# Hybrid attention layer on one core: the last unit's accumulating transfers issued with its evacuation, scan operands loaded later, a low-rank tail in four steps

## The chip, the cores and the metric

The kernel runs on one core of a Trainium2 chip. The metric is the device time of one execution in microseconds (us). The matrix engine is called PE (PEld is its loading of weights), the vector engine DVE, the scalar engine ACT, the GpSimd engine POOL, and the engine that only issues transfers here SP. L12 is line 12 of the kernel before.

## What is computed

One encoder layer over 512 tokens of width 2048, all in float32:

```
h = rmsnorm(x);  proj = h @ w_in              # 2048 x 6176
aq, ak, av, gq, gk, gv, gr, glr = split(proj)
attn = sum over 3 dilation patterns of windowed attention, 16 heads x 64
log_a = log_sigmoid(glr @ gate_w + gate_b) / 16    # low rank: 16 per direction
o = gated_linear_scan(gq, gk, gv, log_a_f) + the same backwards, 4 heads
gla = rmsnorm(o) * norm_w * silu(gr)
x = x + concat(attn, gla) @ w_out
x = x + (silu(h2 @ w_gate) * (h2 @ w_up)) @ w_down;  final rmsnorm
```

## The kernel before

Every float32 product is made of three PE matmuls of rounded parts (high x high, high x low, low x high). So each weight half and each activation is split: ACT casts the high part (L237 for weights) and DVE subtracts to get the low part (L218).

All engines' instruction streams are written in one order by hand; each engine executes its own stream in order, and waits are put in by tile. Small tiles of 512 columns (`s2`, 36 of them, "a" in the profile) and large ones of 1024 (`s4`, 33, "b") are handed out first in, first out; a tile that is handed out again makes its writer wait until the last user of it is done. `s2.free.rotate(14)` puts the 14 most recently freed first.

The stages around the change:

- **The first projection** (`Front.run`): 14 units (gate, scan q/k, attention q/k columns of `w_in`), each of four pieces q = 0 to 3, computed by a seven-product scheme into seven PSUM banks. After a unit's last piece `evac7` is a generator: its first step copies and adds the banks into `c` and three leftovers r1, r2, r3 (L1562 to L1570 and the adds through L1556, L1557); its second step adds once more (L1556 again, the line of the helper) and lets POOL issue four accumulating transfers that add r1, r2 and r3 onto `c` (L1581 to L1584; the last two touch halves that the first two write, and so wait for them); then it idles some turns and `finish` scales the unit by the norm (L1683) and stores it to `qkd`, `grd` or `gfd` from POOL (L1684). The last unit's `finish` is kept aside as `fr.late`.
- During the last unit, piece 1 issues `read_qk(0)` (eight POOL transfers of q and k of the first head pair, L569), and piece 2 issues `gla_operands`: the low-rank weights from SP, and two gate matrices (memset L792, transfer L793) and two reset rows (L794) from POOL.
- **The next jobs** (`run_job`) are ordinary projections, first that of a part of the scans' q and k: 16 weight halves i = 0 to 15, two to a loaded piece, each used for four output blocks, with 12 matmuls for each half (L337 to L339). At most three pieces are held in order of issue; SP loads them (L209). Between the blocks, a credit of 3.1 turns for a half runs the side work, one step at a turn: `run_urgent` first gives the oldest entry of the list `urgent` one step, and then the first entry of `side` gets one.
- `side` begins with `slow(low_rank())` and then `attention()`. `slow` doubles every step. `low_rank` splits the low-rank weights, multiplies in four steps (L818, L819), and in the step of the last eight matmuls also does the whole tail: copy from PSUM (L825), add (L826), scale (L827), and `stacked`, that is two casts on ACT (L800) and a subtraction on DVE (L801). Two more steps do `stacked` for the two gate matrices.
- `attention()` walks 64 units (16 heads x 4 blocks of queries), two steps for a unit: scores (L630, L631), bias added and maximum (DVE L640, which writes a small tile), exponential (ACT L648), scaling (L653 on DVE, L657 on ACT), transposes (PE L662), rounding (ACT L670) and low part (DVE L676), and the product with the values (L686, L687). Bias lines come by SP (L552), values by SP in `load_v` (L600), q and k are rounded by `load_qk` (ACT L592, DVE L588).
- Then the linear-attention scans, the output projection and the feed-forward part.

The hook `before_first(i)` of the first job inserts `load_qk(0)` at half 1, `load_v(0)` at half 2 and `fr.late()` at half 9.

Of the kernel before, what the change touches and what calls it, by code (L numbers as in the profile page):

```python
# [112 lines left out]
def put(*slots):  # L113
    for s in slots:
        if s.home is not None:
            s.home.free.append(s.i)


def layer(nc, tc, x, attn_norm_w, w_in, rel_table, gw_f, gb_f, gw_b, gb_b, gla_norm_w, w_out,
# [7 lines left out]
    with tc.manual_schedule(), \  # L127
# [9 lines left out]
        def hilo(keep=0):  # L137

            if len(s2.free) >= 2 + keep and (len(s2.free) >= 2 * len(s4.free) or not s4.free):
                return s2.get(F32R), s2.get(F32R)  # L140
            return s4.pair()
# [120 lines left out]
        urgent = deque()  # L262

        def run_urgent():
            while urgent:
                try:
                    next(urgent[0])
                    break
                except StopIteration:
                    urgent.popleft()  # L270
# [289 lines left out]
        def read_qk(pr):  # L560

            f = 1 - pr % 2
            if pr < NH // 2:
                qkr[pr] = [[s2.get(F32R) for _ in range(2)] for _ in range(2)]
                for i in range(2):
                    for n in range(2):
                        src = qkd[pr // 2 * 2 + i][64 * n:64 * n + 64, f * 512:(f + 1) * 512]
                        for r in (slice(0, 64), slice(64, 128)):
                            pool.dma_start(out=qkr[pr][i][n].f[r], in_=src)  # L569
# [26 lines left out]
        def load_v(half, ts=range(4)):  # L596
            for t in ts:
                v = s4.get(F32R, [P, 8, 2, DH])
                VS.setdefault(half, []).append(v)
                sp.dma_start(out=v.f.rearrange("p h s c -> p (h s c)"), in_=vd[4 * half + t])  # L600
# [111 lines left out]
        def attention():  # L712


            def run(f, u, n=UNITS):
                if 0 <= u < n:
                    f(u)

            for u in range(UNITS + 7):
                h = u // 4  # L720
                if u < UNITS:
                    if u % 8 == 1:
                        read_qk(h // 2 + 1)
                    if u % 8 == 4 and h // 2 + 1 < NH // 2:
                        urgent.append(slow(load_qk(h // 2 + 1)))
                    while h // 2 not in ready:
                        run_urgent()
                run(att_scores, u)
                run(att_scale, u - 3)
                run(att_round, u - 4)  # L730
                run(att_exp, u - 1)
                if u % 2:
                    run(att_lift, (u - 7) // 2, UNITS // 2)
                mixed = None
                if "mix" in at:
                    pr = at.pop("mix")
                    f, (hi, lo) = mixf.pop(pr), s4.pair() if pr > 4 else hilo()
                    act.copy(hi.t, f.t)
                    mixed = pr, f, hi, lo
                yield  # L740
                run(att_norm, u - 2)
                run(att_transpose, u - 3)
                if u % 2 == 0:
                    run(att_av, (u - 6) // 2, UNITS // 2)
                run(att_rest, u - 4)
                run(att_max, u)
                if u % 2:
                    run(att_mix, (u - 7) // 2, UNITS // 2)
                if mixed:
                    pr, f, hi, lo = mixed  # L750
                    dve.tensor_tensor(lo.t, f.t, hi.f, op=OP.subtract)
                    put(f)
                    mixh[pr] = hi, lo
                if 34 <= u < 37:
                    load_v(1, ((0,), (1,), (2, 3))[u - 34])
                if u == UNITS - 3:
                    load_gla(0)
                yield
# [17 lines left out]
        def slow(steps):  # L776
            for _ in steps:
                yield
                yield


        G = {}
# [3 lines left out]
        def gla_operands():  # L786
            G["raw"] = s2.get(F32, [P, KT, 32])
            sp.dma_start(out=G["raw"].t, in_=w_in[:, C_LR:C_LR + 32].rearrange("(k p) c -> p k c", p=P))
            G["gw"] = [s2.get(F32, [32, 512]) for _ in range(2)]
            G["res"] = [s2.get() for _ in range(2)]  # L790
            for d, w in enumerate((gw_f[0], gw_b[0])):
                pool.memset(G["gw"][d].t, 0.0)  # L792
                pool.dma_start(out=G["gw"][d].t[16 * d:16 * d + 16], in_=w)  # L793
                pool.dma_start(out=G["res"][d].t, in_=c_resets[d:d + 1].to_broadcast([P, S]))  # L794

        def stacked(f, his, at_):

            o = s2.get(F32R, [96, 512])
            for i in his:
                act.copy(o.t[32 * i:32 * i + 32], f.t)  # L800
            dve.tensor_tensor(o.t[32 * at_:32 * at_ + 32], f.t, o.f[0:32], op=OP.subtract)  # L801
            put(f)
            return o

        def low_rank():

            raw = G.pop("raw")
            w = [s2.get(F32R, [P, 8, 64]) for _ in range(2)]
            for i in range(2):
                r = raw.t[:, i * 8:(i + 1) * 8]  # L810
                act.copy(w[i].t[:, :, 0:32], r)
                dve.tensor_tensor(w[i].t[:, :, 32:64], r, w[i].f[:, :, 0:32], op=OP.subtract)
            put(raw)
            yield
            b = ps.get()
            for k in range(KT):
                hi, lo = hT[k]
                mm(b.t[0:64], w[k // 8].t[:, k % 8], hi.t, start=k == 0, stop=False)  # L818
                mm(b.t[0:64], w[k // 8].t[:, k % 8], lo.t, start=False, stop=k == KT - 1)  # L819
                if k % 4 == 3 and k < KT - 1:  # L820
                    yield
            put(*w)
            t = s2.get(F32, [32, 512])
            lr = s2.get(F32, [32, 512])
            act.copy(t.t, b.t[32:64])  # L825
            dve.tensor_tensor(lr.t, b.t[0:32], t.t, op=OP.add)  # L826
            dve.tensor_tensor(lr.t, lr.t, rb[1].t[0:32], op=OP.mult)  # L827
            put(b, t)
            G["lr"] = stacked(lr, (0, 2), 1)
            yield  # L830
            for d in range(2):
                G["gw"][d] = stacked(G["gw"][d], (0, 1), 2)
                yield

        gqd = dr.tile([4, P, 512], F32, name="gqd")
        gfd = dr.tile([2, P, 1024], F32, name="gfd")
# [387 lines left out]
        def gstart():  # L1224
            side.append(slow(low_rank()))
            side.append(attention())

        def before_first(i):
            if i == 1:
                urgent.appendleft(load_qk(0))  # L1230
            if i == 2:
                load_v(0)
            if i == 9:
                fr.late()

        n_front = len(jobs)
# [426 lines left out]
        class Front(Feed):  # L1663
# [29 lines left out]
            def run(self):  # L1693
                banks = {}
                for i, (u, q) in enumerate(self.seq):
                    banks.setdefault(u, [])
                    self.load()
                    self.split(i)
                    self.sums(i + 1)
                    self.sums(i + 2)  # L1700
                    self.split(i + 1)
                    if u == len(self.units) - 1 and q < 3:
                        st.until, st.limit = in_pieces, q + 1
                        st.load()
                    while 2 * q + 1 not in xi:
                        run_side(1)
                    if u == len(self.units) - 1 and q == 3:
                        st.split(jobs[n_front].first + 2)
                    self.products(i, banks[u])
                    if u == len(self.units) - 1:  # L1710
                        for p in (2 * q, 2 * q + 1):
                            put(*xi.pop(p)["slots"])
                        if q == 1:
                            read_qk(0)
                        if q == 2:
                            gla_operands()
                    done = None
                    if q == self.per - 1:
                        if u == len(self.units) - 1:
                            s2.free.rotate(14)  # L1720
                        done = self.evac7(u, banks.pop(u))
                        next(done)
                    run_urgent()
                    if done:
                        urgent.append(done)
# [470 lines left out]
```

## Time and profile before

| | us |
|---|---|
| median of 3 runs | 2165.88 (2165.84 to 2169.17) |
| the profiled execution, its own time | 2164.24 |
| its span | 2162.5 |
| PE busy | 2146.7 |
| DVE, ACT, POOL busy | 1847.4, 1231.2, 361.5 |

Rows of a timeline give start, duration, engine, line, operation, output<-input and count; a bracket behind them is the time the engine stood idle just before, and what released it. Idle time of an engine that isn't the bottleneck costs nothing by itself. "a", "b" and "ps" are small tiles, large tiles and PSUM banks.

### The profile page before, as it was taken

To read this page: it belongs to the slowest core of one execution; us is meant where nothing else is said; L and a number is where in the kernel's file an instruction comes from. 1 tells how busy PE (TensorE), PEld (TensorE's weight loads), DVE (VectorE), ACT (ScalarE), POOL (GpSimd) and SP (SyncE) were. 2 spreads that over 40 slices of the span, in tenths; PEclk is the share of its full clock that TensorE was granted. 3 is DMA by queue.
4 is the path that set the end of the run, shared out by engine and by line. 5 is a ranking of instruction groups with operands and counts; after the bars stand their busy time and mean duration, and the time that the engine had idled before them with its cause. 6 is when DMAs were issued, how large, how long until landed. Compare 5 with 4: busy or idle time off the path is not lost.

```text
span 2162.5 us, 35088 instructions
## 1 busy us (share of the span) xinstructions
PE 2146.7 (99%) x12714; PEld 1896.1 (88%) x12714; DVE 1847.4 (85%) x3195; ACT 1231.2 (57%) x2242; POOL 361.5 (17%) x501
## 2 busy tenths in 40 slices
PE   9999999999999999999999999999999999999998
PEld 7888888788888889888888888888888899999987
DVE  6699998688878788899899998998989888888885
ACT  8455555577776446455555555555555655555562
POOL 0011212311011110021122111211122120021300
PEclk9999999999999999999999999999999999999999
DMA  6477778856565773566777667776776985576982
GB/s 203 137 180 181 180 185 191 230 160 180 165 221 184 259 239 108 150 176 176 188 178 195 174 180 188 180 184 180 182 193 172 266 211 177 178 181 156 284 308 78
DMA packets 265691, 407.55 MB, mean 188 GB/s; under 512 B 19309, under 2 KB 163613, under 8 KB 265518
## 3 DMA queue, kind: packets, MB, share of 16 engines
q1 hardware_dynamic: 206238, 274.59, 40.2%
q0 software_dynamic: 58960, 130.19, 27.5%
q8 instruction: 100, 1.64, 0.3%
q14 instruction: 73, 0.60, 0.1%
q10 hardware_dynamic: 320, 0.53, 0.1%
HBM read 287.47 MB, written 66.39 MB: 164 GB/s over the span
## 4 chain that ended last, share of the span: by engine, by line
PE 58%; DVE 0%; DMA 0%; issue 0%; ACT 0%; DVEq 0%; ACTq 0%
PE ps L1536 24%; PE ps L1522 12%; PE ps L1899 5%; PE ps L1898 5%; PE ps L1897 5%; PE ps L346 1%; PE ps L347 1%; PE ps L348 1%; PE ps L2094 1%; PE ps L2093 1%; PE ps L2092 1%; DMA gd<-b 0%; DVE b L1445 0%; DVE a L2125 0%; DVE a L1556 0%
## 5 line engine op out<-in xcount | busy, mean ns | idle before, releaser
L1440 ACT CAST b<-b 128x1024 fp32r<-128x1024 f32 (+1 forms) x585 | 534.1, 944 | 387.4 <-DVE b L1445 199.3
L1445 DVE TENSOR_TENSOR b<-b,b 128x1024 fp32r<-128x1024 f32 (+1 forms) x585 | 613.7, 1084 | 30.7 <-ACT b L1440 19.5
L1536 PE MATMUL ps<-b,b 128*128 128x512 f32 x1708 | 500.7, 393 | 0.4 <-ACT b L1440 0.2
L1536 PE MATMUL ps<-a,b 128*128 128x512 f32 x1428 | 418.6, 393 | 0.0
L1536 PEld LDWEIGHTS ps<-b,b 128*128 128x128 f32 x1708 | 289.5, 188 | 32.5 <-ACT b L1440 0.7
L1522 PEld LDWEIGHTS ps<-b,b 128*128 128x128 f32 x1708 | 280.6, 190 | 40.8
L1522 PE MATMUL ps<-b,b 128*128 128x256 f32 x1708 | 307.4, 280 | 0.0
L1522 PEld LDWEIGHTS ps<-a,b 128*128 128x128 f32 x1428 | 236.9, 189 | 38.0 <-DVE b L1445 0.5
L1536 PEld LDWEIGHTS ps<-a,b 128*128 128x128 f32 x1428 | 238.6, 189 | 23.5
L1522 PE MATMUL ps<-a,b 128*128 128x256 f32 x1428 | 256.5, 280 | 0.1
L1427 DVE TENSOR_TENSOR b<-b 128x512 f32<-128x512 f32 x268 | 183.4, 684 | 18.1 <-PE ps L1899 6.8
L1897 PE MATMUL ps<-b,b 128*128 128x256 f32 x624 | 176.6, 283 | 0.0
L1898 PE MATMUL ps<-b,b 128*128 128x256 f32 x624 | 176.6, 283 | 0.0
L1899 PE MATMUL ps<-b,b 128*128 128x256 f32 x624 | 176.6, 283 | 0.0
L346 PE MATMUL ps<-b,b 128*128 128x512 f32 x348 | 140.5, 404 | 0.1
L348 PE MATMUL ps<-b,b 128*128 128x512 f32 x348 | 136.1, 391 | 0.1
L347 PE MATMUL ps<-b,b 128*128 128x512 f32 x348 | 135.8, 390 | 0.0
L1428 DVE TENSOR_TENSOR b<-b,b 128x256 f32<-128x256 f32 x268 | 114.0, 425 | 9.3
L1429 DVE TENSOR_TENSOR b<-b,b 128x256 f32<-128x256 f32 x268 | 114.0, 425 | 9.2
L1897 PEld LDWEIGHTS ps<-b,b 128*128 128x128 f32 x624 | 119.8, 192 | 0.0
L1898 PEld LDWEIGHTS ps<-b,b 128*128 128x128 f32 x624 | 119.8, 192 | 0.0
L1899 PEld LDWEIGHTS ps<-b,b 128*128 128x128 f32 x624 | 119.8, 192 | 0.0
(307 smaller groups left out, 4014.6 us busy)
## 6 DMA issues: line engine op xcount, KB each, us to landing
b<-in_w_gate_dram SPq DMA_DIRECT2D x109, 512.0 KB, 3.9
b<-in_w_up_dram SPq DMA_DIRECT2D x88, 512.0 KB, 3.8
b<-in_w_down_dram SPq DMA_DIRECT2D x88, 512.0 KB, 5.9
b<-in_w_in_dram SPq DMA_DIRECT2D x86, 512.0 KB, 3.9
b<-a POOLq DMA_DIRECT2D x168, 256.0 KB, 4.5
b<-in_w_out_dram SPq DMA_DIRECT2D x32, 512.0 KB, 4.8
gd<-b POOLq DMA_DIRECT2D x22, 512.0 KB, 3.9
b<-gd SPq DMA_DIRECT2D x22, 512.0 KB, 8.2
```

The lines of the kernel that those rows point to most:

```text
L346: mm(o, xh.t[:, c], wh.t[:, w], start=first and not on, stop=False, skip_group_check=on)
L347: mm(o, xh.t[:, c], wl.t[:, w], start=False, stop=False, skip_group_check=on)
L348: mm(o, xl.t[:, c], wh.t[:, w], start=False, stop=last, skip_group_check=on)
L1427: dve.tensor_tensor(s_[:, :, 0:2], r[:, :, 1:3], r[:, :, 0:1].to_broadcast(shape), op=OP.add)
L1428: dve.tensor_tensor(s_[:, :, 2], s_[:, :, 0], r[:, :, 2], op=OP.add)
L1440: act.copy(o, src)
L1445: dve.tensor_tensor(o, src, h, op=OP.subtract)
L1522: mm(o, wl, xh, start=False, stop=end, skip_group_check=True)
L1536: mm(o.rearrange("p (s t) -> p s t", s=2), wh, x_, start=first and p == 0, stop=False, skip_group_check=True)
L1897: mm(o, xh[:, t], wh, start=first and h == 0, stop=False, skip_group_check=True)
L1898: mm(o, xh[:, t], wl, start=False, stop=False, skip_group_check=True)
L1899: mm(o, xl[:, t], wh, start=False, stop=last, skip_group_check=True)
```

## The change

- The last unit of the first projection runs the second step of `evac7` right behind the first, so its last add and its four accumulating transfers stand in program order at the unit's end. Other units are as before.
- `gla_operands` keeps only the low-rank weights. Gate matrices and reset rows go into `scan_operands`, called in unit 47 of the attention; the rounding of the gate matrices becomes `gate_weights`, put into `urgent` (doubled by `slow`) in unit 55.
- `stacked` becomes a generator with a step between its casts and its subtraction. The tail of `low_rank` has a step behind the copy, one behind the scale and one inside `stacked`: four steps in all.
- `load_v(0)` moves from half 2 to half 4, `fr.late()` from half 9 to half 7.

```
                 if 34 <= u < 37:
                     load_v(1, ((0,), (1,), (2, 3))[u - 34])
+                if u == 47:
+                    scan_operands()
+                if u == 55:
+                    urgent.append(slow(gate_weights()))
...
         def gla_operands():
             G["raw"] = s2.get(F32, [P, KT, 32])
             sp.dma_start(out=G["raw"].t, in_=w_in[:, C_LR:C_LR + 32].rearrange("(k p) c -> p k c", p=P))
+
+        def scan_operands():
             G["gw"] = [s2.get(F32, [32, 512]) for _ in range(2)]
             G["res"] = [s2.get() for _ in range(2)]
...
-        def stacked(f, his, at_):
+        def stacked(name, f, his, at_):
             o = s2.get(F32R, [96, 512])
             for i in his:
                 act.copy(o.t[32 * i:32 * i + 32], f.t)
+            yield
             dve.tensor_tensor(o.t[32 * at_:32 * at_ + 32], f.t, o.f[0:32], op=OP.subtract)
             put(f)
-            return o
+            G[name] = o
...
             act.copy(t.t, b.t[32:64])
+            yield
             dve.tensor_tensor(lr.t, b.t[0:32], t.t, op=OP.add)
             dve.tensor_tensor(lr.t, lr.t, rb[1].t[0:32], op=OP.mult)
             put(b, t)
-            G["lr"] = stacked(lr, (0, 2), 1)
-            yield
+            yield
+            yield from stacked("lr", lr, (0, 2), 1)
+
+        def gate_weights():
             for d in range(2):
-                G["gw"][d] = stacked(G["gw"][d], (0, 1), 2)
+                yield from stacked(d, G["gw"][d], (0, 1), 2)
                 yield
+            G["gw"] = [G.pop(d) for d in range(2)]
...
-            if i == 2:
+            if i == 4:
                 load_v(0)
-            if i == 9:
+            if i == 7:
                 fr.late()
...
                         done = self.evac7(u, banks.pop(u))
                         next(done)
+                        if u == len(self.units) - 1:
+                            next(done)
```

## The prediction

> **What bounds the kernel now.** I read the page first: how long, and which engine is full.
>
> ```profile
> span 2162.5 us, 35088 instructions
> PE 2146.7 (99%) x12714; PEld 1896.1 (88%) x12714; DVE 1847.4 (85%) x3195; ACT 1231.2 (57%) x2242; POOL 361.5 (17%) x501
> ```
>
> PE is the bound, with 15.8 us of its span idle in all. A change of waits can win some of that and no more; a change that opens a hole in PE loses the hole. Next the table of stages around the first attention units, five stretches of 100 us (columns: PE, PEld, DVE, ACT, POOL busy, then granted clock, DMA share, GB/s).
>
> ```profile
> 300.00:400.00 100.00, 99.02 (x539) 83.62 (x539) 81.59 (x129) 50.75 (x88) 26.11 (x37) 1.00 0.85 217
> 400.00:500.00 100.00, 98.71 (x541) 83.37 (x540) 83.98 (x200) 75.87 (x162) 25.50 (x47) 1.00 0.55 152
> 500.00:600.00 100.00, 99.83 (x563) 84.90 (x562) 82.59 (x199) 77.82 (x165) 10.51 (x20) 1.00 0.59 181
> 600.00:700.00 100.00, 98.00 (x493) 82.12 (x492) 78.32 (x152) 65.08 (x138) 18.61 (x35) 1.00 0.64 211
> 700.00:800.00 100.00, 98.84 (x473) 82.47 (x472) 78.07 (x174) 48.50 (x117) 15.01 (x28) 1.00 0.76 253
> ```
>
> The seam lies in the first two rows: 0.98 + 1.29 = 2.27 us idle. The clock is at 1.00 throughout, so it explains nothing. Then the timeline of PE, where a bracket names what it waited for.
>
> ```profile
> 394.68 0.39 PE L339 MATMUL ps<-b,b 128*128 128x512 f32 x1
> ...
> 395.81 0.39 PE L338 MATMUL ps<-b,a 128*128 128x512 f32 x1
> ...
> 397.19 0.50 PE L339 MATMUL ps<-b,a 128*128 128x512 f32 x1 [0.98 <-DVE a L218]
> ...
> 397.53 0.40 PE L337 MATMUL ps<-b,a 128*128 128x512 f32 x1
> ...
> 409.63 0.39 PE L339 MATMUL ps<-b,a 128*128 128x512 f32 x1
> 410.54 0.66 PE L662 MATMUL ps<-idn,a 128*128 128x128 f32 x4 [0.53 <-ACT a L657]
> ...
> 418.41 0.39 PE L339 MATMUL ps<-b,a 128*128 128x512 f32 x1
> 419.57 0.50 PE L630 MATMUL ps<-a,a 128*128 128x512 f32 x1 [0.77 <-DVE b L676]
> 419.91 0.40 PE L631 MATMUL ps<-a,a 128*128 128x512 f32 x1
> ```
>
> Five matmuls start between 394.68 and 395.81: 0.23 us apart when PE runs free. Three times the distance is longer. At 395.81 the next start is 1.38 us off (1.15 lost, and 0.11 more at the restart, 397.19 to 397.53); at 409.63 it is 0.91 (0.68 lost); at 418.41 it is 1.16 (0.93 lost, restart 0.11). That is 2.98 us. The brackets alone give 0.98 + 0.53 + 0.77 = 2.28, which is the table's idle time of these 200 us: there is no other stall in them. [...]
>
> **Part one: the low-rank tail in steps.** Why did L218 (the low part of a weight half) come late?
>
> ```profile
> 393.04 0.58 ACT L825 COPY a<-ps 32x512 f32<-32x512 f32 x1 [3.26 <-PE ps L819]
> 393.65 0.68 DVE L826 TENSOR_TENSOR a<-ps,a 32x512 f32<-32x512 f32 x1 [1.10 <-ACT a L825]
> 394.36 0.68 DVE L827 TENSOR_TENSOR a<-a,a 32x512 f32<-32x512 f32 x1
> ...
> 395.08 1.26 ACT L800 CAST a<-a 32x512 fp32r<-32x512 f32 x2 [1.46 <-DVE a L827]
> ...
> 396.44 0.69 DVE L218 TENSOR_TENSOR a<-b,a 128x512 fp32r<-128x512 f32 x1
> ```
>
> DVE executes in order. All of the low-rank tail (copy, add, scale, two casts, subtract L801) is issued in one step behind the last low-rank matmuls, so L218 stands behind a chain that changes engine four times, from 393.04 to 396.44. PE reaches the third matmul of its next weight half at 396.04 and has to wait. In the change the copy, the add with the scale, the casts and the subtraction are four steps, and the wrapper doubles each, so that a weight half's L218 is issued between the copy and the add. What DVE has ahead of it then ends at about 391.9 (below), and L218 ends near 392.6, 3.4 us before PE asks. The first stall goes: -1.26 us. Late next is the following half's L218, behind L826 and L827 (395.04) and due one half, 12 matmuls of 0.23 us, later (398.8): on time. The number of steps ahead of the attention stays at fourteen, the fifteenth still starting unit 0, since the two operands' four steps leave the list just as the tail gains four.
>
> **Part two: the last unit's accumulating transfers.** They are the r1, r2, r3 transfers of L1581 to L1584. Before, they are issued only when the last unit's generator gets its second turn, behind the first q/k rounding and the unit before.
>
> ```profile
> 381.13 0.52 POOL L569 DMA_DIRECT2D a<-qkd  x1 [3.10 <-DMA b<-a]
> ...
> 393.11 0.91 POOL L1581 DMA_DIRECT2D b<-a  x1 [0.32 <-issue]
> ...
> 402.87 0.86 POOL L1583 DMA_DIRECT2D b<-a  x1 [7.95 <-DMA b<-a]
> 403.42 1.20 POOL L1584 DMA_DIRECT2D b<-a  x1
> ```
>
> ```profile
> 378.64 0.69 DVE L218 TENSOR_TENSOR a<-b,a 128x512 fp32r<-128x512 f32 x1 [1.67 <-ACT a L237]
> ...
> 391.86 0.68 DVE L1556 TENSOR_TENSOR b<-b,a 128x512 f32<-128x512 f32 x1
> ...
> 407.81 0.69 DVE L640 CUSTOM_DVE_ANT_0 a<-ps,b 128x512 f32<-128x512 f32 x1 [3.81 <-DMA b<-a]
> ...
> 415.70 1.22 DVE L1683 TENSOR_TENSOR b<-b,a 128x1024 f32<-128x1024 f32 x1
> ```
>
> L640 is the third unit's maximum; its output tile is one of r1 to r3, still being read by an accumulating transfer, and DVE stands for 3.81 us. That made the second stall (the scaled probabilities L657 come late), and the third follows from it: DVE works off its backlog while the late scaling L1683 adds 1.22 us at 415.70, just ahead of the L676 that holds PE. In the change the transfers follow the evacuation in program order. "At once" isn't literal: POOL still has the eight q/k reads L569 ahead, the last of them held until 381.13. So L1581 goes at about 381.13 + 0.52 = 381.65, 11.5 us earlier than 393.11. With the same wait for the first two, L1583 follows at 391.4, and what ended DVE's wait at 407.81 ends at 396.3. The third maximum could start at 407.81 - 3.81 = 404.0, or 402.7 with the first stall gone: 6.4 us to spare. Their add (0.68 us at L1556) moves from 391.86 to about 378, where DVE waits 1.67 us for a cast ahead of the L218 at 378.64: nothing. The second stall goes, -0.68.
>
> The late scaling moves from weight half 9 to half 7, by my count some 8 us earlier than 415.70, to about 406 to 407 on the new clock. Its transfers have landed 10 us before, and it falls where DVE stood idle before. So the third stall goes too, -0.93 - 0.11. This is the softest term: 1.22 us on DVE between two maxima can hold PE there as it did here. Bounds 0 to +1.04 (it only moves); I take +0.1, because the backlog is gone. The store of the unit before stands on POOL behind the accumulating chain now, which ends there at about 393, against 392 at the earliest before (it follows that unit's scaling, 1.22 us on DVE, and is ahead of the L1581 at 393.11); the head pairs that read it come last: nothing.
>
> [...]
>
> ```profile
> DMA packets 6934, 8.96 MB, mean 299 GB/s; under 512 B 2590, under 2 KB 5224, under 8 KB 6933
> ...
> b<-vd SPq DMA_DIRECT2D x4, 512.0 KB, 12.3
> b<-line SPq DMA_DIRECT2D x3, 448.0 KB, 12.9
> a<-qkd POOLq DMA_DIRECT2D x8, 128.0 KB, 10.1
> ```
>
> [...] Brought in are 3 x 256 + 128 = 896 KB, taken out are the scan operands' 2 x 256 + 64 = 576 KB: 0.32 MB net, 1.1 us at 299 GB/s, and only behind the q/k reads. L218's 3.4 us cover it: nothing. [...]
>
> **Part three: scan operands and their rounding late.** Removed here: two memsets and four transfers on POOL, four casts on ACT and two subtractions on DVE. They come back in units 47 (POOL) and about 57 to 61 (ACT, DVE).
>
> ```profile
> L800 ACT CAST a<-a x6: 613/618/622, 395.1 to 399.3; 32x512 fp32r<-32x512 f32 x6
> ...
> L801 DVE TENSOR_TENSOR a<-a,a x3: 683/683/685, 395.7 to 399.3; 32x512 fp32r<-32x512 f32 x3
> ...
> L640 DVE CUSTOM_DVE_ANT_0 a<-ps,b x64: 671/681/693, 400.7 to 598.3; 128x512 f32<-128x512 f32 x64
> ```
>
> Units are (598.3 - 400.7) / 63 = 3.14 us apart, so unit 57 is at 580. The cost is 4 x 0.618 = 2.5 us of ACT and 2 x 0.683 = 1.4 us of DVE in some 12 us, in four spaced steps. The row of 500 to 600 leaves ACT 22 us and DVE 17 us free, 2.7 and 2.1 in 12. What is queued behind a cast is the exponential and the rounding of the next unit, and PE waits for those. Bounds: 0, and 2 x 1.15 if each operand holds PE as the tail did in the first stall; no gain, since PE idles 0.17 us in those 100. I take +0.2: q/k rounding, done by then, put bursts of that kind on both engines every eighth unit and PE hardly noticed.
>
> **Part four: values two halves later.** Their four loads move behind one weight piece on SP's queue.
>
> ```profile
> 373.30 2.44 SPq L600 DMA_DIRECT2D b<-vd  x4
> 376.51 2.60 SPq L209 DMA_DIRECT2D b<-in_w_in_dram  x4
> 379.20 4.69 SPq L552 DMA_DIRECT2D b<-line  x1
> ...
> 398.75 0.89 SPq L209 DMA_DIRECT2D b<-in_w_in_dram  x2
> ```
>
> SP runs far ahead (these are issued 20 us before PE's matmuls of those halves), so the change swaps neighbours: a piece first, values at about 375. Landing after 12.3 us, they are there 25 us before the first use, which comes after 410. The first bias line L552 stays last at about 379, landing near 392 to 397, due at 399.4 (unit 0's maximum, at 400.7 before, less the first stall). Nothing.
>
> **Sum.** -1.26 - 0.68 - 1.04 + 0.1 + 0.2 = -2.7 us. The profiled execution took 2164.24 (span 2162.5 and 1.7 around it) and becomes 2161.5; the median of the runs shown is 1.64 above it, 2165.88, and becomes 2163.2.
>
> **Rivals.** *A, waits replaced:* the late scaling costs its 1.04 at half 7, or the chain on POOL stretches beyond its 6.4 us so that the wait at L640 stays. In favour: the transfers still stand behind eight reads, one held 3.10 us. Against: the spare time. Only the first stall goes, less the casts: -1.26 + 0.2 = -1.1, 2164.8. This is also what is left if "at once" does not do what it says.
>
> *B, slower:* SP's queue is in order, and the first bias line now has the four value loads nearer ahead of it. If their tiles aren't free at 375 but only when the last piece of this job gets its own (the L209 at 398.75), L552 is issued near 401 and lands after 12.9 us, at 414, 14 us after 399.4. By the order of the steps PE has about 6 us of matmuls of its own between a unit's scores and its transposes, so it would lose some 8: -1.3 + 8 = +6.7, 2172.6. It decides where the line lands later than about 405. Against: the four tiles and the piece's trade places in one row of free tiles, and at 376.51 the last of those was free.
>
> *C, more than the seam:* 3.16 us idle between 600 and 800 depends on how attention's end, the scans and the output projection lie to each other; earlier and less backlog could halve it: -2.7 - 1.6 = -4.3, 2161.6. In favour: nothing in particular; against: the order there isn't touched.
>
> **How the numbers follow.** Forecast 0.62, A 0.16, B 0.12, C 0.10. 0.2% is 4.3 us, about what a measurement of this kernel can tell from no change: three runs here span 3.3. Forecast and A lie inside that, except 0.04 of the forecast by scatter; C counts as faster. So faster 0.14, same 0.74, slower 0.12. The range runs from 2160.8 (C, with 0.8 of scatter) to 2167.5 (no gain at all, and the 1.64 by which runs differ); it leaves out B.
>
> **What would show it.** Right: no bracket "DVE a L218" on PE near 396, no "DMA b<-a" ahead of L640, L1581 near 382 on POOL, the rows of 300 to 500 together below 0.6 us idle, the row of 500 to 600 below 0.5. Wrong: a PE wait behind L1683 near 406 (A), L640 waiting for the line's transfer near 400 (B), or a PE hole near 575 to 595 behind the casts; and if the seam is closed and the time has moved by more than 4 us, something downstream did it.

## The result and the profile after

The changed kernel takes 2162.77 us (median of 19 runs, 2161.2 to 2164.96), the kernel before 2166.34 beside it (19 runs, 2164.45 to 2169.81). The ratio is 0.9983 with a 95% interval of 0.9975 to 0.999: 3.7 us faster, 2.2 to 5.4. The forecast was 2163.2 and 2.7 us. One of the eleven runs of the row "late scaling at half 9" below took 2631 us, at a granted clock of 0.75; that row's median counts it, its ratio doesn't.

The profiled execution took 2162.97 us, span 2161.2. Its table of stages, for the five stretches shown of before (columns as there: PE, PEld, DVE, ACT, POOL busy, then clock, DMA share, GB/s):

```profile
300.00:400.00 100.00, 99.07 (x541) 83.91 (x541) 81.63 (x130) 49.28 (x86) 25.39 (x36) 1.00 0.82 209
400.00:500.00 100.00, 100.00 (x554) 85.19 (x553) 84.59 (x202) 76.11 (x163) 22.82 (x44) 1.00 0.56 166
500.00:600.00 100.00, 99.83 (x559) 84.70 (x558) 83.72 (x199) 80.77 (x172) 14.05 (x26) 1.00 0.60 179
600.00:700.00 100.00, 98.01 (x493) 82.14 (x492) 78.41 (x153) 65.12 (x139) 18.59 (x35) 1.00 0.63 208
700.00:800.00 100.00, 98.84 (x473) 82.47 (x472) 78.72 (x175) 48.54 (x117) 15.34 (x29) 1.00 0.76 252
```

From 400 on the idle 1.29 us are gone, and nothing behind the seam has changed. The 0.93 left in the first row aren't the seam's. A finer table, of before and then of after, shows where they lie:

```profile
200.00:360.00 160.00, 160.00 (x921) 140.46 (x920) 149.04 (x240) 86.58 (x144) 32.65 (x40) 1.00 0.74 180
377.00:425.00 48.00, 45.72 (x218) 35.36 (x217) 30.48 (x64) 27.71 (x59) 17.68 (x31) 1.00 0.87 251
```

```profile
200.00:360.00 160.00, 158.57 (x909) 138.91 (x909) 146.91 (x235) 84.44 (x141) 32.64 (x40) 1.00 0.74 179
377.00:425.00 48.00, 48.00 (x235) 38.27 (x234) 31.60 (x67) 27.84 (x61) 16.73 (x30) 1.00 0.93 265
```

The seam, 377 to 425, went from 2.28 us idle to none. In this one execution PE also lost 1.43 us between 200 and 360, where both kernels do the same; over all profiles of this study that stretch lost 0 to 2.27 us, whatever the kernel. So the two profiled executions differ by only 1.3 us while the medians differ by 3.6, and everything in the seam is some 1.8 us later on the changed kernel's clock. In the following, the idle time of PE in the seam is the sharp measure (45.72 of 48 is 2.28 idle), and the times, with intervals of about 0.0018, are the blunt one.

The order on DVE and ACT around the low-rank tail, and the transfers on POOL, in the profile after (L832 is the copy, L834 the add, L835 the scale, L806 and L808 casts and subtraction; L1592 to L1595 the accumulating transfers, L1694 the scaling and L1695 the store of a unit, the row at 405.72 being the late one):

```profile
394.88 0.58 ACT L832 COPY a<-ps 32x512 f32<-32x512 f32 x1 [1.93 <-PE ps L826]
394.91 0.68 DVE L218 TENSOR_TENSOR b<-b,b 128x512 fp32r<-128x512 f32 x1
395.51 0.67 DVE L834 TENSOR_TENSOR a<-ps,a 32x512 f32<-32x512 f32 x1
396.22 0.68 DVE L835 TENSOR_TENSOR a<-a,a 32x512 f32<-32x512 f32 x1
396.82 0.67 DVE L218 TENSOR_TENSOR a<-b,a 128x512 fp32r<-128x512 f32 x1
...
397.87 0.39 PE L339 MATMUL ps<-b,b 128*128 128x512 f32 x1
```

```profile
384.39 0.52 POOL L569 DMA_DIRECT2D a<-qkd  x1 [2.92 <-DMA b<-a]
385.62 0.93 POOL L1592 DMA_DIRECT2D b<-a  x1 [0.71 <-DMA a<-qkd]
386.34 1.12 POOL L1593 DMA_DIRECT2D b<-a  x1
396.98 0.86 POOL L1594 DMA_DIRECT2D b<-a  x1 [9.51 <-DMA b<-a]
397.53 1.21 POOL L1595 DMA_DIRECT2D b<-a  x1
398.07 1.22 POOL L1695 DMA_DIRECT2D qkd<-b  x1
398.62 3.29 POOL L569 DMA_DIRECT2D a<-qkd  x5
403.68 0.52 POOL L569 DMA_DIRECT2D a<-qkd  x1 [1.77 <-DMA b<-a]
```

```profile
405.10 0.69 DVE L640 CUSTOM_DVE_ANT_0 a<-ps,b 128x512 f32<-128x512 f32 x1 [0.59 <-PE ps L631]
...
405.72 1.22 DVE L1694 TENSOR_TENSOR b<-b,a 128x1024 f32<-128x1024 f32 x1
```

The next half's L218 stands ahead of the add and ends at 395.6; PE takes that half's low part first at 397.87. The third maximum (405.10) waits for its scores, for no transfer. But the accumulating chain is not where the forecast put it: L1594 waits 9.51 us and goes at 396.98, and POOL still waits for it at 403.68. That last wait isn't for a tile. In this trace POOL's 486 transfers signal eight semaphores in turn, and none of the 478 that have another eight places before them went until that one had landed. Eight places before this read stands L1594, with L1595, the store and five reads between, and it landed at 403.39. In the same way L1592 waits 0.71 us, till 385.62, for the first of the eight q and k reads ahead of it, which landed at 385.05. All this asked for experiments.

### The profile page after: what moved, and what is told of

Same layout as the page of the kernel before. It is cut to its first block, busy times and chain, and to the rows that moved or that the text cites. A ratio compares the mean times of both kernels' runs of the same rounds, so it can differ in the third digit from the quotient of the medians.

```text
span 2161.2 us, 35082 instructions
## 1 busy us (share of the span) xinstructions
PE 2146.3 (99%) x12714; PEld 1896.3 (88%) x12714; DVE 1847.9 (86%) x3195; ACT 1230.7 (57%) x2242; POOL 361.8 (17%) x501
## 4 chain that ended last, share of the span: by engine, by line
PE 94%; DVE 3%; DMA 1%; ACT 1%; issue 1%; POOL 0%; DVEq 0%; SPq 0%; ACTq 0%
PE ps L1547 32%; PE ps L1533 16%; PE ps L348 6%; PE ps L346 6%; PE ps L347 6%; PE ps L1911 5%; PE ps L1912 5%; PE ps L1910 5%; PE ps L662 1%; DMA b<-a 1%; PE ps L687 1%; PE ps L686 1%; PE ps L630 1%; PE ps L339 1%; PE ps L337 1%; PE ps L338 1%
## 5 line engine op out<-in xcount | busy, mean ns | idle before, releaser
L1547 PE MATMUL ps<-b,b 128*128 128x512 f32 x1708 | 500.7, 393 | 0.4 <-ACT b L1451 0.2
L346 PE MATMUL ps<-b,b 128*128 128x512 f32 x332 | 133.8, 403 | 0.0
L348 PE MATMUL ps<-b,b 128*128 128x512 f32 x332 | 129.8, 391 | 0.0
L347 PE MATMUL ps<-b,b 128*128 128x512 f32 x332 | 129.5, 390 | 0.0
```

What stands on the lines that cost most here:

```text
L346: mm(o, xh.t[:, c], wh.t[:, w], start=first and not on, stop=False, skip_group_check=on)
L347: mm(o, xh.t[:, c], wl.t[:, w], start=False, stop=False, skip_group_check=on)
L348: mm(o, xl.t[:, c], wh.t[:, w], start=False, stop=last, skip_group_check=on)
L1547: mm(o.rearrange("p (s t) -> p s t", s=2), wh, x_, start=first and p == 0, stop=False, skip_group_check=True)
```

## The experiments

Each time is the median of 11 runs, with 32 or 33 runs of the kernel before beside each set (2166.2 to 2166.8). "Idle" is that of PE in the profile's seam, of one execution each. The first four rows, the next four and the last four were taken in three sets, the last on another chip; rows of different sets are compared by their ratios.

| kernel | us | ratio to before | idle 377 to 425 |
|---|---|---|---|
| transfers alone | 2164.02 | 0.9992 [0.9983, 1.0001] | 0.98 |
| tail alone | 2164.81 | 0.9992 [0.9984, 1.0001] | 2.70 |
| places back, first | 2163.34 | 0.9987 [0.9978, 0.9995] | 1.91 |
| tail in one step | 2164.29 | 0.9988 [0.9979, 0.9997] | 0.99 |
| the changed kernel again | 2162.86 | 0.9983 [0.9974, 0.9992] | 0 |
| places back, second | 2162.65 | 0.9981 [0.9972, 0.999] | 0.87 |
| gate rounding in a burst | 2162.93 | 0.9983 [0.9974, 0.9993] | 0 |
| operands early | 2164.92 | 0.9992 [0.9984, 1.0001] | 0.79 |
| values at half 2 | 2162.85 | 0.9982 [0.9973, 0.9991] | 0 |
| late scaling at half 9 | 2162.28 | 0.9979 [0.997, 0.9988] | 0 |
| tiles held, on before | 2165.66 | 0.9994 [0.9985, 1.0002] | 2.69 |
| tiles held, places back | 2162.78 | 0.9982 [0.9973, 0.9991] | 0 |

**The parts one by one.** The kernel before with the transfers alone:

```
                         next(done)
+                        if u == len(self.units) - 1:
+                            next(done)
```

> The kernel before with one part of the change: the last unit's second step directly behind the first. Theory (three stalls, two causes: the low-rank tail ahead of L218 makes the first, the accumulating transfers that still read a tile which the third maximum wants make the second and third): the first stall near 396 stays with 1.15 us between starts beyond the usual 0.23, the wait of L640 for a transfer and the two later stalls are gone; 0.68 + 0.93 + 0.11 = 1.7 us less than before, ratio 0.9992. Rival (tiles: what helps is the four small tiles that the scan operands no longer hold, so that the third maximum gets another tile): the wait of L640 stays or moves to a neighbouring unit, and the time is that of before within 0.5 us.

Idle 0.98, all of it the first stall (PE waited for L218 once, 0.98 us); the second and third are gone, and the ratio 0.9992 is the one expected. But it isn't the order alone, for DVE still waits for a transfer there:

```profile
405.48 0.69 DVE L218 TENSOR_TENSOR a<-b,a 128x512 fp32r<-128x512 f32 x1 [1.88 <-DMA b<-a]
```

With the second step earlier, r1 to r3 are also given back earlier, and r3 is handed to a weight half in place of the third maximum. The wait has moved to that half's L218, and there it costs PE nothing.

The changed kernel without its early transfers:

```
                         next(done)
-                        if u == len(self.units) - 1:
-                            next(done)
...
-            if i == 4:
+            if i == 2:
                 load_v(0)
-            if i == 7:
+            if i == 9:
                 fr.late()
```

> The changed kernel with the transfers put back (second step on its later turn, values at half 2, late scaling at half 9): only the low-rank tail in steps and the scan operands late. Theory: the first stall is gone (1.26 us), the wait of L640 for a transfer of some 3 to 5 us stays, and with it the second and third stall; 1.1 us less than before, ratio 0.9995. Rival (tiles): with four more free tiles the third maximum gets a tile that no transfer reads, the wait of L640 is gone without the transfers being moved, and the kernel is as fast as the changed one, 2.7 to 3.6 us less than before, ratio 0.9984 to 0.9988.

Neither. The first stall is gone and, as the rival had it, L640 waits for no transfer; but the seam lost 2.70 us all the same. ACT, POOL and then PE in the timeline:

```profile
405.02 0.86 POOL L1594 DMA_DIRECT2D b<-a  x1 [7.76 <-issue]
405.56 1.21 POOL L1595 DMA_DIRECT2D b<-a  x1
406.11 5.00 POOL L569 DMA_DIRECT2D a<-qkd  x8
```

```profile
411.23 0.63 ACT L592 ACTIVATE a<-a 128x512 fp32r<-128x512 f32 x1 [2.14 <-DMA a<-qkd]
413.72 0.63 ACT L592 ACTIVATE a<-a 128x512 fp32r<-128x512 f32 x1 [1.35 <-DMA a<-qkd]
```

```profile
416.72 0.66 PE L662 MATMUL ps<-idn,a 128*128 128x128 f32 x4 [1.18 <-ACT a L657]
420.55 0.50 PE L630 MATMUL ps<-a,a 128*128 128x512 f32 x1 [1.52 <-DVE b L676]
```

The second head pair's q and k reads stand on POOL behind the late chain (406.11), their rounding L592 waits on ACT, and the scaling L657 queued behind it holds PE. With the attention running earlier (third maximum at 404.18, not 407.81) and the chain a little later (L1594 at 405.02, not 402.87), this is late next. It is what the early transfers remove, besides the tile.

The changed kernel with the tail in one step:

```
             act.copy(t.t, b.t[32:64])
-            yield
             dve.tensor_tensor(lr.t, b.t[0:32], t.t, op=OP.add)
...
-            yield
-            yield from stacked("lr", lr, (0, 2), 1)
+            for _ in stacked("lr", lr, (0, 2), 1):
+                pass
+            for _ in range(3):
+                yield
```

> The changed kernel with the low-rank tail in one step again (copy, add, scale, casts and subtraction together, then three empty steps so that the attention starts where it did); transfers early, operands late, places as changed. Theory: the first stall returns, 1.1 to 1.3 us between a second and a third matmul near 397 and 0.1 at the restart, and nothing else; 1.26 us more than the changed kernel. Rival (the four casts of the gate matrices on ACT made the first stall, not the chain of the tail): no stall returns, since these casts stay late, and the time is that of the changed kernel within 0.4 us.

```profile
398.50 0.69 DVE L218 TENSOR_TENSOR b<-b,b 128x512 fp32r<-128x512 f32 x1
...
399.24 0.50 PE L339 MATMUL ps<-b,b 128*128 128x512 f32 x1 [0.99 <-DVE b L218]
```

The first stall is back with 0.99 us and nothing else is, though the gate matrices' casts stay late: the chain of the tail makes it. The ratio is 0.9988 against 0.9983 of the changed kernel in the next set, some 1.1 us more; their intervals overlap, so the times don't show it and the profile does.

**Which tile a maximum gets.** The kernel with both places put back:

```
-            if i == 4:
+            if i == 2:
                 load_v(0)
-            if i == 7:
+            if i == 9:
                 fr.late()
```

> The changed kernel with the two places put back: values loaded at half 2, late scaling at half 9; the transfers stay early. Theory: without a backlog on DVE the late scaling finds room at half 9 as at half 7, and the values are early in both; at most 0.3 us more than the changed kernel, ratio to before 0.9984 to 0.9987, PE idle between 377 and 425 below 0.3 us. Rival (the place of the late scaling is what made the third stall): a PE wait of 0.8 to 1.0 us for L676 returns near 417, 1.0 us more than the changed kernel.

The execution that its profile caught took 2167.6 us and had lost 2.27 us of PE already between 200 and 360. It shows a wait of 4.43 us at L640, the third stall, and the first stall, though the tail is in steps:

```profile
398.48 0.69 DVE L588 SCALAR_TENSOR_TENSOR a<-a,a 128x512 fp32r<-128x512 f32 x1 [0.90 <-ACT a L592]
399.09 1.22 DVE L1694 TENSOR_TENSOR b<-b,a 128x1024 f32<-128x1024 f32 x1
400.23 0.69 DVE L218 TENSOR_TENSOR a<-b,a 128x512 fp32r<-128x512 f32 x1
...
400.97 0.50 PE L339 MATMUL ps<-b,a 128*128 128x512 f32 x1 [1.03 <-DVE a L218]
```

Nothing of the tail stands ahead of this L218. The q and k reads came some 4 us later by the clock than in the profile after (first rounding L592 at 390.41 against 386.13), and their rounding L588 and the scaling of the unit before (L1694) held DVE. It was run again beside the changed kernel:

> The kernel with values at half 2 and late scaling at half 9 again, since its first profile was of an execution whose transfers were slow from the start (2167.6 us against a median of 2163.3). Theory (that execution's crowding, not the places, brought the stalls): this profile has q and k reads that land within 11 us of the first issue, no first stall, no DMA wait ahead of L640, PE idle between 377 and 425 below 0.5 us. Rival (values two halves earlier crowd the q and k reads each time): the first q/k rounding again waits for its read till 12 us or more after the first issue, the first stall is back with about 1 us, 1 us more than the changed kernel.

> The changed kernel once more, beside the others of this set. Both theories: ratio to before 0.998 to 0.999, PE idle between 377 and 425 at most 0.3 us. If it shows the wait for q and k reads and a first stall as the profile of the kernel with the places put back did, the seam's margin is smaller than one profile of each says.

```profile
405.56 0.69 DVE L640 CUSTOM_DVE_ANT_0 a<-ps,b 128x512 f32<-128x512 f32 x1 [4.68 <-DMA b<-a]
...
419.14 0.50 PE L630 MATMUL ps<-a,a 128*128 128x512 f32 x1 [0.78 <-DVE b L676]
```

No first stall this time, so the places don't make it; but here the expectation failed: DVE waits 4.68 us for a transfer at L640, with L1594 issued at the same time as in the changed kernel (397.30 against 397.04 in its second profile). The third stall is back behind it, 0.78 of the 0.87 idle. The early order alone doesn't free the maximum. What does is which small tile it is handed, and the program's free lists settle that. In the kernel before, r3, which the last transfer reads, goes to the third maximum. In this one it goes to the second: 405.56 is the second L640 of the attention. In the changed kernel a weight half gets r3 and needs it later, and the third maximum gets a tile of the same evacuation that no transfer reads. Four more large tiles free at half 2 and 3, or four more small ones, shift that by a few places, since weight halves take whichever size is more plentiful. The same kernel with the operands loaded early:

```
-                if u == 47:
-                    scan_operands()
...
                             gla_operands()
+                            scan_operands()
```

> The changed kernel with only the loading of the scan operands put back to piece 2 of the last unit (their rounding stays late): four memsets and transfers more ahead of the accumulating ones on POOL, four small tiles fewer to hand out, 576 KB more in the crowded stretch. Theory (the transfers' issue order closes the seam, the tiles don't): the chain on POOL is 4 to 5 us later, which its spare time covers, PE idle between 377 and 425 below 0.4 us, 0 to 0.4 us more than the changed kernel. Rival (tiles and POOL's room are part of what closes it): a wait of L640 or of the second q/k rounding for a transfer of 1 us or more is back, PE idle 1 us or more.

```profile
406.31 0.69 DVE L640 CUSTOM_DVE_ANT_0 a<-ps,b 128x512 f32<-128x512 f32 x1 [5.06 <-DMA b<-a]
```

The rival holds as to the wait: four small tiles fewer, and r3 goes to the second maximum again. The idle time is 0.79 us and not the 1 us or more that it asked for (0.69 of it at a late L657), and the time is 2.1 us above the changed kernel of the same set; where the rest comes from isn't shown.

Then each place by itself, and the tile by itself. Values at half 2, late scaling at 7:

```
-            if i == 4:
+            if i == 2:
                 load_v(0)
```

> The changed kernel with only the values loaded at half 2 again (late scaling stays at half 7). Theory now (tiles: a maximum waits where it is handed the tile r3 that the last accumulating transfer reads; with the values taken two halves earlier fewer large tiles are free, weight halves take small ones sooner, and r3 falls to the third maximum again): L640 waits 4 to 5 us for a transfer as in the kernel with both places put back, PE idle between 377 and 425 of 0.5 to 1.5 us, 0 to 1 us more than the changed kernel. Rival (the early order of the transfers alone frees L640): no DMA wait at L640, idle below 0.2.

```profile
403.14 0.69 DVE L640 CUSTOM_DVE_ANT_0 a<-ps,b 128x512 f32<-128x512 f32 x1 [1.91 <-DMA b<-a]
```

The DMA wait is back as the tile theory says, at the second maximum and not the third, and only 1.91 us long (L1594 went at 394.85 here). That much DVE makes good: idle 0. The miss in the size is the point: a wait of 1.91 us cost PE nothing here, and behind those of 4.68 and 5.06 us above it lost 0.78 and 0.69 us.

```
-            if i == 7:
+            if i == 9:
                 fr.late()
```

> The changed kernel with only the late scaling at half 9 again (values stay at half 4). Theory now (tiles): r3 goes to a weight half as in the changed kernel, L640 has no DMA wait, PE idle between 377 and 425 below 0.3 us, the time of the changed kernel within 0.4 us. Rival (the place of the late scaling makes the third stall): PE waits 0.8 us for L676 near 419 as in the kernel with both places put back.

No wait, idle 0, 2162.28 us. Where the late scaling stands did not matter where no maximum waited (idle 0 with it at half 7 and at half 9). When one waited 4.4 to 5.1 us, PE lost 0.7 to 0.8 us behind it, at L676 with the scaling at half 9 and at L657 with it at half 7. Now the tiles of the last unit are given back only with its late scaling:

```
-                put(r1, r3, t, r2, v)
+                if u == len(self.units) - 1 and self.wide == 0:
+                    put(t, v)
+                    self.held_r = r1, r3, r2
+                else:
+                    put(r1, r3, t, r2, v)
...
                     put(c_)
+                    if u == len(self.units) - 1:
+                        put(*self.held_r)
```

> The kernel with both places put back and the tiles r1, r2, r3 held until the late scaling. Theory now: L640's wait of 4 to 5 us is gone, PE idle between 377 and 425 below 0.3 us, the time of the changed kernel within 0.4 us, which shows that the places work through the tiles alone. Rival (the late scaling's place counts by itself): a PE wait for L676 of 0.8 us stays.

Idle 0 in place of 0.87, no wait at L640: as expected, the places work through the tiles. The times (2162.78, and 2163.34 and 2162.65 without holding) can't tell 0.9 us apart.

The same edit on the kernel before:

> The kernel before with one edit: the tiles r1, r2, r3 of the last unit are given back only with its late scaling, so that nobody can be handed one earlier; the transfers stay late, all else as before. Theory now (two locks: the tile, and the second pair's q and k reads that stand on POOL behind the late chain): the wait of L640 is gone, but the q/k rounding L592 on ACT waits 2 us or more for its reads near 409, and PE idles 1 to 2.5 us between 400 and 425, beside the first stall's 0.98; the time of before within 0.7 us. Rival (the tile alone made the second and third stall): idle between 400 and 425 below 0.3 us, 1.7 us less than before, without moving a transfer.

The rival holds as far as the second and third stall go: none between 400 and 425, without moving a transfer. Its 1.7 us in the time aren't shown (ratio 0.9994, interval 0.9985 to 1.0002). The reads of the second pair, on POOL at 407.12, were in time, with the attention itself later behind a long first stall, so how they would fare without that stall stays open. PE's timeline, then the stages (columns as above):

```profile
396.61 0.39 PE L338 MATMUL ps<-b,a 128*128 128x512 f32 x1
399.68 0.50 PE L339 MATMUL ps<-b,a 128*128 128x512 f32 x1 [2.69 <-DVE a L218]
...
401.30 0.63 PE L339 MATMUL ps<-b,a 128*128 128x512 f32 x1
401.73 0.63 PE L337 MATMUL ps<-b,a 128*128 128x512 f32 x1
```

```profile
399.00:401.00 2.00, 1.32 (x6) 1.10 (x7) 1.60 (x3) 1.95 (x4) 0.00 (x0) 1.00 1.07 334
401.00:405.00 4.00, 4.00 (x12) 3.14 (x11) 2.48 (x5) 2.18 (x5) 0.00 (x0) 0.57 1.00 260
405.00:410.00 5.00, 5.00 (x23) 4.14 (x23) 3.22 (x9) 2.60 (x6) 3.97 (x8) 1.00 0.58 96
```

The q and k reads of the first pair landed later than in the profile of before (first L592 at 386.30 against 383.05), their rounding on DVE pushed the tail's add to 396.16 (393.65 before) and L218 to 398.94 (396.44): a hole of 3.07 us between two starts. Behind it the granted clock fell to 0.57 for four us, with matmuls 0.43 us apart instead of 0.23 for about eight of them, another 1.6 us (8 x 0.20).

**The late rounding.** The changed kernel with the four casts and two subtractions of the gate matrices in one step:

```
             for d in range(2):
-                yield from stacked(d, G["gw"][d], (0, 1), 2)
-                yield
+                for _ in stacked(d, G["gw"][d], (0, 1), 2):
+                    pass
+            yield
```

> The changed kernel with the rounding of the gate matrices in one step of unit 57 or so: four casts on ACT and two subtractions on DVE in a row instead of four spaced steps. Theory (the cover is real but works by spacing, cost 0.2 us in four steps): 4 x 0.618 = 2.5 us of ACT at once hold the exponential and the rounding of one unit, PE waits 0.7 to 1.5 us between 573 and 595, 0.5 to 1.3 us more than the changed kernel. Rival (there is room for any of it): PE waits less than 0.3 us, same time.

Stages of before, of after and of the burst, in this order:

```profile
560.00:620.00 60.00, 59.55 (x328) 50.54 (x328) 45.16 (x101) 45.95 (x94) 7.66 (x14) 1.00 0.59 193
```

```profile
560.00:620.00 60.00, 59.55 (x329) 50.57 (x328) 45.85 (x101) 48.86 (x99) 7.64 (x14) 1.00 0.62 202
```

```profile
560.00:620.00 60.00, 59.36 (x324) 50.11 (x324) 44.45 (x98) 49.40 (x99) 7.62 (x14) 1.00 0.63 205
```

Idle 0.45, 0.45 and 0.64 us. ACT has the 2.9 us more (48.86 against 45.95) and PE doesn't notice; even the burst costs only 0.19. The rival holds: the room is there.

## Why the prediction was right

**Three stalls in the seam, 2.98 us, all removable: right.** The seam's idle time is none in both profiles of the changed kernel, against 2.28 before. Two of the signs named ahead failed as they were written, without touching this: the rows of 300 to 500 lost 0.93 us and not under 0.6, all of it ahead of the seam, and the first accumulating transfer went at 385.62 and not near 382.

**The tail in steps, -1.26: right**, in mechanism and in size for a quiet execution (putting the step back brings 0.99 idle; 1.15 and 0.11 between starts had been read off before). The spare time was 2.3 us (L218 ends at 395.6, PE wants it at 397.87) and not 3.4, since the q and k reads kept DVE later. Mis-sized is what the stall costs in other executions: with those reads later it grew from 0.98 us of idle time to 2.69 in the kernel before with tiles held, and the lower clock behind it took 1.6 more. And it can come back with the tail in steps, 1.03 us in the first profile of the places put back, when the same reads are late enough. The profile of before didn't show that. The forecast of 2.7 us lies inside the measured interval of 2.2 to 5.4. The size of the stall can account for the measured gain being nearer to 3.7 than to 2.7 us, and for the runs of before lying 2 us above its own profile; this is argued, since only one execution of before itself was traced.

**The transfers, "11.5 us earlier, 6.4 to spare": wrong step, right outcome, by luck.** The part failed first at "L1581 goes at about 381.65": on a clock 1.8 us later it went at 385.62, since it also had to wait for the first of the eight reads to land. It failed again at "with the same wait for the first two": L1594 waited 9.51 to 10.36 us, not 7.95, behind a last q/k read held to 384 and not 381, and goes 5.9 us earlier than before by the clock, 396.98 against 402.87. Next to nothing was left to spare: r3's last reader L1595 landed at 404.4 (issued at 397.53, 6.9 us), 0.7 us ahead of the third maximum, and a second maximum that is handed r3 waits 1.91 to 5.06 us with the transfers early too. What frees L640 is the tile it gets, which the prediction didn't look at: in the changed kernel, moving the operands and the values, which it entered as a cost and as nothing, hands r3 to a weight half. What the early order does is to give r3 back sooner, in the free list and by the clock, and to let the second pair's reads go first, at 398.62 instead of 404.10; without it the seam loses 2.70 us by another way.

**The late scaling at half 7, the "softest term", +0.1: it was 0**, at half 7 and at half 9. The third stall came from the wait at L640, not from the scaling's place. "Landed 10 us before" was wrong: the last of its transfers landed at 404.4, 1.3 us ahead of the scaling at 405.72.

**The casts late, +0.2: it was 0**; bounds of 0 to 2.3 were far too wide on the high side. **Values two halves later, "nothing": wrong as to the reason.** Their landing cost nothing, but taking four large tiles later is one of the two things that hand r3 to a weight half in the changed kernel; the other is the four small tiles that the late operands leave free.

Of the rivals, A did not come (no DVE backlog, nothing behind L1694), though its condition that the chain on POOL outgrows the spare time nearly did, B did not (the line's transfers held no maximum), C neither: idle in 600 to 800 is 3.15 against 3.16 us.

## What to carry to other kernels

Where tiles are handed out first in, first out, a wait for a transfer at some far instruction says only that this instruction drew the tile. Look up who draws it before and after an edit: moving any allocation by a few places, or holding the tile back, can remove the wait or move it to where there is room (with the transfers alone, 3.81 us at L640 became 1.88 us at a weight half's L218, at no cost to PE). And split a chain that changes engines several times into steps with the steady work between them, since what stands behind the chain on its engine waits for the slowest hand-over, by an amount that varied from one execution to another: PE waited 0.98 us for the L218 behind it in the profile of before, 2.69 in that of before with tiles held.

## What was not expected of the hardware

In the one execution with a hole of 3.07 us between two starts of PE, that of before with tiles held, the granted clock was 0.57 from 401 to 405 us behind it, and matmuls started 0.43 us apart there against 0.23. Behind the holes of 1.9 us and less in the seams of the other profiles it was 1.00. That the hole brought the lower clock isn't shown by one execution.

In the crowded stretch (DMA share 0.87 between 377 and 425 in the profile of before, 0.74 between 200 and 360; the prediction's rows of transfers are of its 370 to 400 us), POOL waited 9.19 to 10.74 us at the third accumulating transfer in ten profiles of kernels that issue them early, against 7.95 in the profile of before. The first two, of 256 KB each, landed after 9.1 and 10.1 us in the profile after, and after 7.2 and 8.6 before. Issued 7.5 us earlier by the clock (385.62 against 393.11), they let the third go only 5.9 us earlier.
